# The recurrence's products pA of two heads, issued in turn into two PSUM tiles

## The chip, the cores and the metric

The kernel runs on one core of one Trainium2 chip. The metric is the time of one execution in device microseconds, the median of several runs; the profiled execution is one more run of the same program. Engines are named as in the profile: PE is TensorE (PEld its weight loads), DVE is VectorE, ACT is ScalarE, POOL is GpSimd and SP is SyncE, which issues the DMAs.

## The reference, cut to what matters

A block of a model with 512 tokens and 1024 channels: a gated feed-forward, a mixer with two branches (an RWKV-7 recurrence with 16 heads of 64, and dilated attention), a second feed-forward, then two more layers of another kind. The change lies in the recurrence, which the reference writes as a scan over the tokens:

```
def step(state, inp):
    r_t, w_t, k_t, v_t, a_t, b_t = inp
    sa = jnp.einsum('bhvk,bhk->bhv', state, a_t)
    state = (state * w_t[:, :, None, :] + sa[..., None] * b_t[:, :, None, :]
             + v_t[..., None] * k_t[:, :, None, :])
    return state, jnp.einsum('bhvk,bhk->bhv', state, r_t)
```

The kernel computes it by chunks of 64 tokens. Within a chunk, all products of the rows (a, r) with the rows (b, k) are needed, masked to the past tokens: this is the matrix A of the chunk, and the part of it that belongs to a and b is inverted.

## The kernel before, in words

The 16 heads are worked in 8 pairs j; a pair's two heads lie on partitions 0 to 63 and 64 to 127 of the same tiles. The 512 tokens are 8 chunks c. In the mixer (`rwkv`, line 1179) five generators run beside one another:

- `rw_chunks` (line 1443), the recurrence itself: for each pair and chunk the short products po, pu, pS and po again, with copies on ACT and an add on DVE between them.
- `rw_solve` (line 1397), the inverse of each chunk's matrix: it loads the masked products through a DRAM tile scrA into AS, runs 31 rows of a DVE multiply (pr) and a DVE sum (Tt), writes the result through scrT, and ends with the products pZ and pW.
- `rw_prep` (line 1269), which makes each pair's operands; the change is here.
- `rw_stream` and `rw_fill` (lines 1241 and 1255), the projections prj of 128x512, three products for each block of weights, which fill TensorE. The norms of attention's q and k (ssq, bcq, pt) hang on them.

A generator's `yield` names the engine that its next step wants. `drive` (line 438) chooses, in a first pass over the program, which generator goes next: the one whose engine is free soonest by a clock of estimated costs (`Clock`, line 192), plus a priority (0 for the recurrence, 300 for the inverse, 600 for the preparation, 2000 and 5000 for the projections). The clock takes a 128-column float32 product at 4 x 128 columns of 2.4 GHz and prices one after the other. The order found is recorded and replayed; a scheduler below it places the instructions on the engines and adds all waits. Each engine runs its instructions in the written order.

In `rw_prep`, BK holds the rows b and k and AR the rows a and r of a pair, 128 partitions with 8 chunks of 128 columns. From line 1345 on the loops run over the head h, then over the half q of the chunks. A step makes the products of four chunks of one head into one PSUM tile pA (128x512, one of the two buffers of tag g, line 1274), and a step on DVE multiplies it by the mask into AA. Tag g also holds pz, pa, pl, psk, prn, pb, pv and pbt of the preparation and ssq, bcq and pt of attention's norms. After the fourth multiply, SP issues the DMAs to scrA and TB (lines 1356 to 1359) and the flag A (line 1362) lets the inverse of the pair begin. From the third pair on, the block waits until the recurrence is done with the pair before the last (line 1340).

Attention, later in the kernel, has products of the same form in `att_block` (line 1119): s is made for the two heads of a pair, from partitions 0 to 63 and from 64 to 127, each into its own PSUM tile.

Of the kernel before, what the change touches and what calls it, by code (L numbers as in the profile page):

```python
# [13 lines left out]
P = 128  # L14
# [513 lines left out]
class K:  # L528
# [740 lines left out]
    def rw_prep(self, j, tw, lad):  # L1269
        nc, t1, t2 = self.nc, self.t1, self.t2  # L1270
# [3 lines left out]
        g = lambda sh, nm: self.rps["g"].tile(sh, F32, tag="g", name=nm)  # L1274
        tri, bd, mask = self.rcon["tri"], self.rcon["bd"], self.rcon["rwmask"]
# [48 lines left out]
        AR = t1.tile([P, 8, P], F32, tag="AR", name="AR")  # L1324
        BK = t1.tile([P, 8, P], F32, tag="BK", name="BK")
# [17 lines left out]
        AAs = AA.rearrange("p h c t -> p (h c) t")  # L1343
        R["AR"] = AR
        pend = None
        for h in range(2):
            p0 = 64 * h
            for q in range(2):
                pA = g([P, 4, P], "pA")
                for x in range(4):  # L1350
                    c = q * 4 + x
                    nc.tensor.matmul(pA[:, x], BK[p0:p0 + 64, c], AR[p0:p0 + 64, c], start=True, stop=True)
                yield "DVE"
                nc.vector.tensor_mul(AA[:, h, q * 4:q * 4 + 4], pA, mask.unsqueeze(1).to_broadcast([P, 4, P]))
                yield "PE"
        for b in range(2):
            nc.sync.dma_start(self.scrA[j][b].rearrange("s j i -> j s i"), AAs[b * 32:b * 32 + 32, :, b * 32:b * 32 + 32])
        R["TB"] = TB = t2.tile([64, 16, P], F32, tag="TB", name="TB")
# [1138 lines left out]
```

## Time and profile before

| | us |
|---|---|
| median of 3 runs | 2564.78 |
| lowest and highest run | 2545.41, 2572.88 |
| the profiled execution | 2555.58 |
| its span, first to last instruction | 2553.8 |
| mean granted TensorE clock, share of full speed | 0.948 |

The page of the profile gives for each engine the busy time and its share of the span, and for 40 equal slices of the span the busy share. The chain of waits is the work that ended last, followed back from the last instruction. A group of instructions has its count, its busy time in us and the mean of one in ns, then the idle time of its engine before it and what ended it. A float32 product shows as two records, each with its weight load.

### The profile page before, as it was taken

How to read it: one execution, taken by the hardware profiler on the slowest of the kernel's cores; microseconds unless marked ns; L12 is line 12 of the kernel's file. 1: busy time of each engine (PE TensorE's matmuls, PEld its weight loads, DVE VectorE, ACT ScalarE, POOL GpSimd, SP SyncE). 2: the span in 40 equal slices, each digit the busy share in tenths (PEclk: the TensorE clock that was granted, in tenths of full speed). 3: DMA queues.
4: the chain of work that ended last, by engine and by line, in shares of the span. 5: the costliest groups of instructions: out<-in, count | busy, mean ns of one | idle time of the engine just before them, and what ended most of it. 6: DMA issues, size and time to landing. Idle time of an engine off the chain costs nothing.

```text
span 2553.8 us, 33817 instructions
## 1 busy us (share of the span) xinstructions
PE 2372.9 (93%) x12556; PEld 1920.0 (75%) x12556; DVE 1703.2 (67%) x3157; ACT 1014.7 (40%) x1852; POOL 745.1 (29%) x441
## 2 busy tenths in 40 slices
PE   8798999999999999989989899999889999789897
PEld 6576887877777777757878788888677778677776
DVE  8999357676666656534767846664559865568865
ACT  4212224334233333335433533333335655345553
POOL 4444443010111110212423233335332332232331
PEclk9998999999889869979999999999899999899998
DMA  6555323433223224332423232433310222310221
GB/s 210 188 199 180 100 95 107 121 86 102 79 56 105 66 56 117 130 121 79 127 96 113 82 128 74 145 109 112 128 61 25 71 63 67 116 47 26 64 78 53
DMA packets 122196, 254.24 MB, mean 100 GB/s; under 512 B 39208, under 2 KB 54576, under 8 KB 121392
## 3 DMA queue, kind: packets, MB, share of 16 engines
q1 hardware_dynamic: 122032, 252.09, 31.6%
q8 instruction: 99, 1.62, 0.3%
q14 instruction: 65, 0.53, 0.1%
HBM read 222.07 MB, written 21.59 MB: 95 GB/s over the span
## 4 chain that ended last, share of the span: by engine, by line
PE 68%; DVE 19%; ACT 4%; issue 4%; DMA 2%; POOL 2%; SPq 0%; DVEq 0%; ACTq 0%; POOLq 0%
PE prj L318 12%; PE po L318 11%; PE pj L318 7%; PE pu L318 6%; PE pg L318 6%; DVE mjunk L318 5%; PE pm L318 4%; PE pwo L318 4%; PE sc L318 3%; PE pt L318 2%; DVE c0cy L318 1%; DVE fb L318 1%; PE pA L318 1%; DMA wm<-in_l_mod 1%; PE pl L318 1%
## 5 line engine op out<-in xcount | busy, mean ns | idle before, releaser
L318 POOL TENSOR_TENSOR wlo<-wraw,whi 128x1024 fp32r<-128x1024 f32 (+5 forms) x239 | 552.3, 2312 | 1012.6 <-ACT whi L318 926.4
L318 ACT CAST whi<-wraw 128x1024 fp32r<-128x1024 f32 (+4 forms) x330 | 324.8, 984 | 584.3 <-PE po L318 110.7
L318 PE MATMUL prj<-HH,whi 128*128 128x512 f32 x464 | 197.4, 426 | 0.0
L318 PE MATMUL prj<-HH,wlo 128*128 128x512 f32 x464 | 190.9, 412 | 0.0
L318 PE MATMUL prj<-HL,whi 128*128 128x512 f32 x464 | 187.4, 404 | 0.0
L318 DVE SCALAR_TENSOR_TENSOR mjunk<-wm,cc 128x1024 f32<-128x1024 f32 x96 | 165.5, 1724 | 6.1 <-DMA wm<-in_l_mod 4.7
L318 PE MATMUL po<-FH,whi 128*128 128x512 f32 x352 | 141.1, 401 | 13.2 <-ACT FH L318 13.1
L318 DVE TENSOR_TENSOR wlo<-wraw,whi 128x512 fp32r<-128x512 f32 (+1 forms) x149 | 122.5, 832 | 41.6 <-ACT whi L318 35.8
L318 PE MATMUL pu<-HH,wlo 128*128 128x512 f32 x352 | 139.0, 401 | 11.9 <-POOL wlo L318 11.9
L318 PE MATMUL pg<-HH,whi 128*128 128x512 f32 x352 | 139.5, 396 | 8.2 <-ACT HH L318 7.3
L318 PE MATMUL pu<-HH,whi 128*128 128x512 f32 x352 | 141.4, 402 | 1.3 <-ACT whi L318 1.3
L318 PE MATMUL po<-FL,whi 128*128 128x512 f32 x352 | 140.2, 398 | 0.8 <-DVE FL L318 0.8
L318 PE MATMUL po<-FH,wlo 128*128 128x512 f32 x352 | 139.8, 397 | 1.1 <-POOL wlo L318 1.1
L318 PE MATMUL pu<-HL,whi 128*128 128x512 f32 x352 | 140.2, 398 | 0.0
L318 PE MATMUL pg<-HL,whi 128*128 128x512 f32 x352 | 139.0, 395 | 0.5 <-DVE HL L318 0.5
L318 PE MATMUL pg<-HH,wlo 128*128 128x512 f32 x352 | 135.8, 392 | 1.1 <-POOL wlo L318 1.1
L318 DVE TENSOR_TENSOR ptl<-pt,pth 128x512 fp32r<-128x512 f32 x156 | 105.1, 685 | 36.3 <-ACT pth L318 35.3
L318 PE MATMUL pj<-HH,whi 128*128 128x512 f32 (+1 forms) x304 | 123.2, 409 | 3.2 <-ACT HH L318 3.2
L318 POOL TENSOR_TENSOR se<-SV,EC 64x128 f32<-64x128 f32 x56 | 36.3, 648 | 302.4 <-DVE SV L318 238.8
L318 PE MATMUL pj<-HL,whi 128*128 128x512 f32 (+1 forms) x304 | 123.4, 407 | 0.6 <-DVE HL L318 0.6
L318 PE MATMUL pj<-HH,wlo 128*128 128x512 f32 (+1 forms) x304 | 123.7, 408 | 0.0
L318 ACT ACTIVATE pr<-sc,am 128x768 f32<-128x768 f32 (+1 forms) x120 | 98.0, 818 | 58.7 <-DVE am L318 54.4
(745 smaller groups left out, 5974.2 us busy)
## 6 DMA issues: line engine op xcount, KB each, us to landing
wraw<-in_ffn_w SPq DMA_DIRECT2D x96, 512.0 KB, 3.3
wm<-in_l_mod SPq DMA_DIRECT2D x48, 512.0 KB, 3.5
wraw<-in_l_b SPq DMA_DIRECT2D x45, 512.0 KB, 3.4
wraw<-in_w_rkv SPq DMA_DIRECT2D x24, 512.0 KB, 3.7
wraw<-in_w_qkv SPq DMA_DIRECT2D x18, 512.0 KB, 3.3
wraw<-in_w_gate SPq DMA_DIRECT2D x16, 512.0 KB, 3.9
wraw<-in_ffn_w SPq DMA_DIRECT2D x16, 448.0 KB, 3.4
xd<-X SPq DMA_DIRECT2D x24, 256.0 KB, 3.0
```

Source lines behind the costliest of these rows:

```text
L318: r = real(*a, **kw)
```

## The change

The loop over the halves q becomes the outer one. Two tiles pA are taken together, one for each head; the products of a chunk are issued for head 0 and then head 1, chunk by chunk; then two steps on DVE multiply the two tiles. All operands, tiles and shapes stay as they are.

```
-        for h in range(2):
-            p0 = 64 * h
-            for q in range(2):
-                pA = g([P, 4, P], "pA")
-                for x in range(4):
-                    c = q * 4 + x
-                    nc.tensor.matmul(pA[:, x], BK[p0:p0 + 64, c], AR[p0:p0 + 64, c], start=True, stop=True)
+        for q in range(2):
+
+            pAs = [g([P, 4, P], "pA") for h in range(2)]
+            for x in range(4):
+                c = q * 4 + x
+                for h in range(2):
+                    p0 = 64 * h
+                    nc.tensor.matmul(pAs[h][:, x], BK[p0:p0 + 64, c], AR[p0:p0 + 64, c], start=True, stop=True)
+            for h in range(2):
                 yield "DVE"
-                nc.vector.tensor_mul(AA[:, h, q * 4:q * 4 + 4], pA, mask.unsqueeze(1).to_broadcast([P, 4, P]))
-                yield "PE"
+                nc.vector.tensor_mul(AA[:, h, q * 4:q * 4 + 4], pAs[h], mask.unsqueeze(1).to_broadcast([P, 4, P]))
+            yield "PE"
```

## Rows read from the trace of the kernel before

**Rows 1.** The page, busy time of each engine over the span
```profile
PE 2372.9 (93%) x12556; PEld 1920.0 (75%) x12556; DVE 1703.2 (67%) x3157; ACT 1014.7 (40%) x1852; POOL 745.1 (29%) x441
```

**Rows 2.** By stretch: length, busy PE, PEld, DVE, ACT, POOL, clock, DMA share, GB/s
```profile
460.00:1076.00 616.00, 594.80 (x3486) 462.11 (x3485) 392.96 (x1185) 209.60 (x413) 76.29 (x87) 0.91 0.31 87
900.00:972.00 72.00, 66.78 (x403) 52.63 (x403) 43.08 (x137) 22.24 (x54) 9.77 (x14) 0.76 0.22 58
```

**Rows 3.** The chain of waits from 460 to 972 us, shares by line
```profile
by line: PE prj L318 41.4%; PE po L318 8.2%; PE pA L318 5.7%; PE pu L318 3.8%; PE pS L318 3.3%; DVE pr L318 2.7%; PE ssq L318 2.6%; PE pb L318 2.1%; PE pgg L318 1.9%; DVE Tt L318 1.9%; DVE wlo L318 1.8%; issue 1.7%; PE pa L318 1.6%; PE pl L
```

**Rows 4.** Groups of instructions of TensorE from 460 to 972 us, pA
```profile
L318 PE MATMUL pA<-AR,BK 64*128 64x128 f32 x256 | 42.9, 312 | 4.5 <-DVE BK L318 2.4 <-DVE AA L318 2.0
```

**Rows 5.** Timeline of TensorE (start us, length us, what), two blocks of pA
```profile
646.31 1.16 PE L318 MATMUL pA<-AR,BK 64*128 64x128 f32 x8
647.40 0.43 PE L318 MATMUL po<-SV,AA 128*128 128x64 f32 x2
...
754.92 2.05 PE L318 MATMUL pA<-AR,BK 64*128 64x128 f32 x16
756.90 0.50 PE L318 MATMUL prj<-HH,whi 128*128 128x512 f32 x1
```

**Rows 6.** Timeline of TensorE, attention's products s: two heads, then one
```profile
1149.36 0.72 PE L318 MATMUL s<-kT,qT 64*128 64x128 f32 x8
1150.01 0.50 PE L318 MATMUL pm<-HH,wlo 128*128 128x512 f32 x1
...
1155.99 0.71 PE L318 MATMUL s<-kT,qT 64*128 64x128 f32 x4
1156.63 0.50 PE L318 MATMUL pm<-HH,wlo 128*128 128x512 f32 x1
```

**Rows 7.** Busy time by stretch, as in Rows 2: the clock around three blocks
```profile
754.90:756.90 2.00, 2.00 (x17) 1.86 (x17) 0.93 (x3) 1.98 (x3) 0.00 (x0) 1.00 0.00 0
1149.30:1150.10 0.80, 0.80 (x11) 0.62 (x9) 0.68 (x2) 0.80 (x4) 0.00 (x0) 1.00 0.00 0
906.30:910.40 4.10, 4.03 (x17) 3.53 (x16) 2.88 (x6) 0.89 (x2) 0.20 (x1) 0.50 0.12 17
```

**Rows 8.** Timeline, the block of pA at 906.28 us
```profile
906.28 4.21 PE L318 MATMUL pA<-AR,BK 64*128 64x128 f32 x16
```

**Rows 9.** Instructions on tile pA: the multiplies, ns min/median/max, first and last start
```profile
L318 DVE TENSOR_TENSOR AA<-pA,c_rwmask x32: 669/684/694, 471.3 to 971.0; 128x512 f32<-128x512 f32 x32
```

**Rows 10.** Timeline around the first and the third pair's multiplies
```profile
471.29 1.28 DVE L318 TENSOR_TENSOR AA<-pA,c_rwmask 128x512 f32<-128x512 f32 x2
...
472.03 2.31 PE L318 MATMUL pA<-AR,BK 64*128 64x128 f32 x16 [0.52 <-DVE AA L318]
...
579.02 0.93 PE L318 MATMUL pA<-AR,BK 64*128 64x128 f32 x6
...
603.09 1.29 DVE L318 TENSOR_TENSOR AA<-pA,c_rwmask 128x512 f32<-128x512 f32 x2 [2.98 <-PE po L318]
...
604.22 0.71 PE L318 MATMUL pA<-AR,BK 64*128 64x128 f32 x4
```

**Rows 11.** Busy time by stretch: first, last and sum of five at low clock
```profile
473.70:477.10 3.40, 3.40 (x11) 2.04 (x10) 1.59 (x3) 0.00 (x0) 0.00 (x0) 0.50 0.25 68
...
746.80:753.50 6.70, 6.70 (x25) 5.08 (x25) 3.65 (x10) 0.94 (x4) 1.18 (x2) 0.50 0.42 141
sum 23.60, PE 22.18 PEld 15.97 DVE 17.08 ACT 2.19 POOL 1.18; mean PE 4.44 PEld 3.19 DVE 3.42 ACT 0.44 POOL 0.24
```

**Rows 12.** Timeline of pZ, first and last of eight; groups of DVE, 460 to 972 us
```profile
549.05 1.13 PE L318 MATMUL pZ<-AS,TB 32*32 32x32 f32 x30
1064.01 1.16 PE L318 MATMUL pZ<-AS,TB 32*32 32x32 f32 x31
...
L318 DVE TENSOR_TENSOR pr<-Tt,AS 128x2 f32<-128x2 f32 (+30 forms) x210 | 75.0, 357 | 4.6
L318 DVE TENSOR_REDUCE Tt<-pr 128x1 f32<-128x2 f32 (+30 forms) x209 | 51.1, 245 | 4.4
```

## The prediction

> **What bounds the kernel now.** I read the page first: over the 2553.8 us span TensorE matmul is busy 93%, VectorE 67%, ScalarE 40% [rows 1]. The products pA lie only between 469 and 970 us, so the second view is the table by stretch. From 460 us to 1076 us, where the last projection of this stage ends, TensorE is busy 594.8 of 616 us and idle for 21 us; VectorE is busy 393 us [rows 2]. In the part from 900 to 972 us the share is lower (66.8 of 72 us) and the granted clock is 0.76. The third view, the chain of waits cut to 460 to 972 us, shows what that busy engine is worth: the projections prj hold 41.4% of the chain, po 8.2%, pA 5.7%, and the VectorE rows of the inverse, pr and Tt, 2.7% and 1.9% [rows 3]. TensorE in its written order is the bound of this stage, and pA is on its path for 5.7% of 512 us = 29.2 us. The groups of instructions put the busy time of all 256 pA records at 42.9 us [rows 4]. The code has 8 pairs of heads x 2 heads x 8 chunks = 128 products, so each is two records.
>
> **The change part by part.** *Added and removed instructions: none.* The 128 products, the 32 mask multiplies and the DMAs of the block stay as they are. What changes is the order, which PSUM buffers are held together, and the steps the planner sees.
>
> *Products in turn.* Today a step issues four products of one head. The timeline shows sixteen records of one head from 754.92 to 756.90 us = 1.98 us until the next instruction, and eight from 646.31 to 647.40 us = 1.09 us; the difference over eight is 0.111 us a record [rows 5]. What do two heads cost that alternate? Attention's products s have the same shape (64 rows, 64x128 moving) and take both halves of the rows into two PSUM tiles. Eight of them, four of each head, stand from 1149.36 to 1150.01 us = 0.65 us; four of a single head, from 1155.99 to 1156.63 us, take 0.64 us [rows 6]. So a second head costs nothing there: the two halves run side by side. The granted clock is 1.00 in the stretches at 754.9 and at 1149.3 us, so these compare like with like [rows 7]. Sixteen records of two heads are eight slots: 0.65 + 4 x 0.111 = 1.09 us, against 1.98 us. That is 0.89 us less for each of 16 groups of sixteen: 14.2 us. At granted clock 0.50 (the 2.4 GHz engine at 1.2 GHz) sixteen records take 4.21 us, a short wait in them included [rows 7, 8]; about two and a half of the 16 groups lie there and save some 0.85 us more each: 2 us, 16.3 us in all. Bounds from both sides: nothing if the halves do not overlap, 21.4 us if all 42.9 us halve. What counts is the path. Half of the chain's 29.2 us is 14.6 us, close to the 14.2 us of the groups; I take 14.5 us.
>
> *The buffers.* Both tiles of a step now come from tag g, which has two. Today the second tile's products lie over the first tile's multiply, and the third tile waits for the first multiply alone. Afterwards the second step's two heads wait for both multiplies. A multiply takes 0.685 us [rows 9]. In the timeline of the first pair, two multiplies start at 471.29 us and the next products at 472.03 us with 0.52 us of idle; for the third pair the first two tiles' products end at 579.95 us, their multiplies run from 603.09 to 604.38 us, and the next products start at 604.22 us, between them other work keeps TensorE busy [rows 10]. Half of the eight pairs are as tight as these two; each would be late by one more multiply: 4 x 0.7 = 2.8 us. Bounds: nothing, if the planner puts projections there as it does now, and for eight pairs both multiplies with a handoff of about 0.2 us on either side (1.8 us each), 14 us. I take 2.8 us, nearest to the two rows.
>
> *A rule that speaks against it.* The row says that two multiplies take 1.37 us, longer than the 1.09 us that sixteen paired products would. The Trainium skill, TensorEngine Tiling (Array Packing), section PSUM Bottleneck, says that tiling quickens TensorE but not the emptying of PSUM, which may then be the limit. By that rule the 32 multiplies, 21.9 us, would set the pace instead of 16 x 1.98 = 31.7 us, and the gross gain would be 9.8 us and not 14.2 us. By the rows of the third pair the multiplies lie far from their products with other TensorE work between, so I keep the larger sum.
>
> *The step order.* Eight alternations of TensorE and VectorE steps become two steps of eight products with two multiplies after each. Head 1's first products move ahead of head 0's second. The scrA and TB DMAs on SP and the inverse still wait for the last multiply, and no POOL work is moved. But the recorded plan, which prices eight products as eight in a row and knows nothing of the overlap, will be another for the whole stage. No row prices that. The idle time of TensorE in the stage, 21 us [rows 2], bounds what a better order can win, and I take the same for a worse one; value zero.
>
> *How much carries through.* TensorE is 97% busy, but at each handoff (po, copy, pu, copy, pS) it waits for others, and a shorter TensorE stretch turns partly into waits. I keep 0.8 of the net: 0.8 x (14.5 - 2.8) = 9.4 us. Bounds are none and all of it.
>
> *Clock.* Five stretches at granted clock 0.50 begin on, or within 1 us after, a block of pA products, 23.6 us in sum [rows 11]. The engine was near fully busy in them, so at full clock about half, 11.8 us, would go. Whether denser products keep the clock up no row tells; I take 2 us and leave the rest as a rival.
>
> Sum: 9.4 + 2 = 11.4 us, so the profiled execution would go from 2555.58 to 2544.2 us. The median of the runs, 2564.78, is 9.2 us above that execution; kept, it gives 2553 us.
>
> **The rivals.** *The clock stays up too.* All 11.8 us come: 9.4 + 11.8 = 21.2 us, 2543.6 us. For it: five blocks of half-empty products stand next to the falls. Against: low clock also falls where the recurrence's short products run, as from 900 to 972 us.
>
> *The inverses set the pace.* Their pZ products start at 549.05 us for the first pair and at 1064.01 us for the last, seven steps of 73.6 us each [rows 12]. If the inverse with its VectorE rows and DMAs paces the stage, TensorE only waits longer, and no more than the tail of 2 us is won: 2563 us. Against: pr and Tt hold 4.6% of the chain, prj 41.4%.
>
> *No overlap.* For the third pair the sixteen products of one head were cut into pieces of 4, 6 and 6 records with recurrence products between; the last piece is in [rows 10]. If the written order separates the heads, nothing is saved and the longer wait remains: 2564.8 + 2.8 = 2568 us.
>
> *Slower: the seam in a pair.* Both buffers of tag g are held until two multiplies are done, and everything else that uses the tag (pb, pv, pz, pa, the norms of q and k) queues behind. If VectorE's order puts these multiplies behind rows of the inverse (0.357 + 0.245 us for one of its 31 rows [rows 12]), as it did for 23 us in the third pair, and TensorE's order has the second step before the filling projections, TensorE stands. It waits in order, so the recurrence behind it stands too. It decides from 14.5 / 8 = 1.8 us a pair. With ten inverse rows, 6 us, at each of eight seams: 48 - 14.5 = 33 us, 2598 us.
>
> **How the numbers follow.** Chances: forecast 0.50, clock 0.20, inverses pace 0.13, no overlap 0.05, seam 0.12. A measurement of this kernel tells about 1% from no change, 25.6 us. Faster by over that needs the clock rival with a kinder plan (0.10 of its 0.20), or a kind plan in the forecast (0.09 of 0.50): 0.19. Slower by over 1% is the seam in most of its cases and hardly anything else: 0.09. The rest, 0.72, lies within. For eight in ten the range goes down to the clock rival with some 17 us of the plan's 21 us (2527 us) and up past "no overlap" by 8 us (2576 us); what is left out is most of the seam above and a very good plan below.
>
> **What would show it.** Right: 256 pA records again, but sixteen of two heads until the next instruction in about 1.1 us at full clock, busy time of the group near 22 to 26 us, its chain share in this stretch near 3%, VectorE's 32 multiplies unchanged at 0.685 us, and the last projection of the stage some 10 us earlier. Wrong: pA records still 0.111 us apart (no overlap); pZ still 73.6 us apart with more TensorE idle than 21 us (inverses pace); TensorE waits for the mask multiply well above 5 us in sum (seam). The forecast itself falls if the stage's end moves by another amount than pA's busy time explains, which would be the new plan or the clock.

## The result, and the profile after

The changed kernel takes 2581.24 us (median of 20 runs, 2570.81 to 2604.05); in the same comparison the kernel before takes 2554.55 us (20 runs, 2542.92 to 2576.46). The ratio is 1.0094 with a 95% interval of 1.0066 to 1.0122: slower by about 24 us (the medians alone are 26.7 us apart), where the forecast was 11.4 us faster and its range ended at 2576 us. The three runs shown ahead of the prediction had a median 10 us above that of these 20; the ratio goes by the 20. The profiled execution takes 2590.40 us with a span of 2588.6 us, 34.8 us longer than before, at a mean granted clock of 0.932 instead of 0.948.

The page of the changed kernel, which answers to [rows 1]: busy time of the engines, then the granted clock (PEclk, in tenths of full speed) in 40 slices of the span, 65 us each.
```profile
PE 2398.7 (93%) x12556; PEld 1935.6 (75%) x12556; DVE 1710.2 (66%) x3157; ACT 1015.1 (39%) x1854; POOL 739.9 (29%) x441
...
PEclk9999999989777776999999999999899999899998
```
The same line of the page of the kernel before:
```profile
PEclk9998999999889869979999999999899999899998
```
The count of TensorE's instructions is the same, 12556, yet they are busy for 25.8 us more. The clock line says where: in the slices from 10 to 15 (counted from 0), some 650 to 1040 us, it stands at 7 and 6, where before it is 8 or 9 but for one 6.

First the part that the change is about. The groups of instructions from 460 to 1000 us, TensorE's pA (against [rows 4]) and VectorE's multiplies:
```profile
L318 PE MATMUL pA<-AR,BK 64*128 64x128 f32 x256 | 34.9, 342 | 0.3 <-DVE AA L318 0.3
...
L318 DVE TENSOR_TENSOR AA<-pA,c_rwmask 128x512 f32<-128x512 f32 x32 | 21.4, 684 | 8.7 <-PE po L318 4.8 <-PE pA L318 3.9
```
The timeline of TensorE after the change (start us, length us): the first block of pA, and then the block of products pZ with which each of the eight inverses ends:
```profile
469.32 1.16 PE L318 MATMUL pA<-AR,BK 64*128 64x128 f32 x16
470.42 0.50 PE L318 MATMUL prj<-HH,whi 128*128 128x512 f32 x1
...
547.25 1.19 PE L318 MATMUL pZ<-AS,TB 32*32 32x32 f32 x32
621.71 1.19 PE L318 MATMUL pZ<-AS,TB 32*32 32x32 f32 x32
698.11 1.91 PE L318 MATMUL pZ<-AS,TB 32*32 32x32 f32 x32
782.27 1.91 PE L318 MATMUL pZ<-AS,TB 32*32 32x32 f32 x32
856.69 1.91 PE L318 MATMUL pZ<-AS,TB 32*32 32x32 f32 x32
933.76 1.91 PE L318 MATMUL pZ<-AS,TB 32*32 32x32 f32 x32 [1.39 <-DVE AS L318]
1003.99 1.91 PE L318 MATMUL pZ<-AS,TB 32*32 32x32 f32 x32 [1.45 <-DVE AS L318]
1079.34 1.19 PE L318 MATMUL pZ<-AS,TB 32*32 32x32 f32 x32
```
Sixteen records of two heads take 470.42 - 469.32 = 1.10 us until the next instruction, where sixteen of one head took 1.98 us [rows 5]: the two halves do run side by side. The group falls from 42.9 to 34.9 us. TensorE waits little for the multiplies, as its waits from 460 to 1090 us show (what waited, for what; us in total, times, longest):
```profile
PE pb L318 <- DVE AA L318: 2.4, 3, 1.3
...
PE pA L318 <- DVE AA L318: 0.3, 1, 0.3
```
In the kernel before the same view has one such row:
```profile
PE pA L318 <- DVE AA L318: 2.0, 2, 1.5
```
So these waits grow by 0.7 us.

Second, the pZ rows tell of the clock too: a block takes 1.19 us where the granted clock is 1.00 (as at 1079 us) and 1.91 us where it is 0.50 (as at 782 us), and five of the eight are long. In the kernel before the eight blocks start at 549.05, 624.66, 697.71, 773.54, 852.05, 920.88, 991.61 and 1064.01 us, and only the one at 852.05 takes 1.91 us. The steps hardly differ, 73.6 us in the mean before [rows 12] and (1079.34 - 547.25) / 7 = 76.0 us after.

What lies between them does differ. The table by stretch after the change (columns as in [rows 2]): from the third pZ to the last, from the last to attention's first products s, and the whole stage.
```profile
698.10:1079.30 381.20, 350.65 (x1925) 265.38 (x1924) 223.48 (x708) 108.94 (x239) 41.82 (x56) 0.77 0.25 67
1079.30:1164.00 84.70, 81.95 (x453) 61.56 (x452) 29.19 (x56) 29.88 (x56) 14.06 (x11) 0.98 0.42 134
440.00:1164.00 724.00, 683.09 (x3756) 521.80 (x3755) 426.61 (x1251) 232.48 (x461) 84.14 (x99) 0.84 0.30 85
```
The same three stretches of the kernel before:
```profile
697.70:1064.00 366.30, 354.25 (x2084) 272.99 (x2084) 227.13 (x696) 121.70 (x254) 45.23 (x56) 0.88 0.30 85
1064.00:1122.70 58.70, 46.61 (x289) 31.47 (x289) 16.28 (x35) 19.99 (x43) 16.43 (x12) 0.88 0.31 105
440.00:1122.70 682.70, 649.42 (x3759) 500.20 (x3758) 420.85 (x1250) 234.16 (x461) 90.55 (x100) 0.90 0.32 90
```
And the first two for the projections prj alone (busy PE, PEld, DVE, ACT of instructions on this tile), after:
```profile
698.10:1079.30 381.20, 158.61 (x552) 109.11 (x552) 4.42 (x6) 17.84 (x29) 0.77 0.25 67
1079.30:1164.00 84.70, 56.33 (x217) 38.64 (x216) 0.00 (x0) 6.83 (x10) 0.98 0.42 134
```
and before:
```profile
697.70:1064.00 366.30, 196.97 (x720) 135.20 (x720) 6.70 (x9) 21.88 (x34) 0.88 0.30 85
1064.00:1122.70 58.70, 12.19 (x49) 8.70 (x48) 0.00 (x0) 2.06 (x3) 0.88 0.31 105
```
Here is where the time came from. Attention begins 41.3 us later (1164.0 against 1122.7 us). The whole span is only 34.8 us longer, but what follows attention's start varies by more than these 6.5 us: two profiles of the kernel before, the second of which is met below, differ there by 8.5 us. Of the 41.3 us, 14.9 lie between the third and the last pZ, which hold 168 projection products *fewer*, and 26.0 behind the last pZ, where these 168 now stand: 217 records against 49, in a place where nothing but one pair's recurrence is left to lie beside them. Over the whole stage TensorE runs the same instructions (3756 and 3759 records) and is busy 33.7 us longer and idle 7.6 us longer. With two levels, 1.00 and 0.50, a mean of 0.84 over 724 us is 232 us at the low one, and 0.90 over 682.7 us is 137 us.

The changed lines move no projection. The written order does: the planner put its steps in another order. The count of prj products in each interval between inverses, in program order, first to last (up to the first pZ, between two, behind the last):
```
before   312  180  132  134  178   72  132  204   48
after    336  158  130  120   96   72   72  192  216
```
Intervals with 72 products and with 204 take about the same time (before: 68.8 us with 72, 72.4 us with 204; after: 77.1 and 70.2 us with 72, 75.4 us with 192). In the timeline the projections start 0.23 us apart at full clock, so 132 of them are some 30 us of TensorE's work (an estimate from these rows), and an interval without them is shorter by a few us or not at all. A projection taken out of an interval is thus hardly a gain there; it is work left for the end.

### The profile page after: what moved, and what is told of

Same layout as the page of the kernel before. It is cut to its first block, busy times and chain, and to the rows that moved or that the text cites. A ratio compares the mean times of both kernels' runs of the same rounds, so it can differ in the third digit from the quotient of the medians.

```text
span 2588.6 us, 33828 instructions
## 1 busy us (share of the span) xinstructions
PE 2398.7 (93%) x12556; PEld 1935.6 (75%) x12556; DVE 1710.2 (66%) x3157; ACT 1015.1 (39%) x1854; POOL 739.9 (29%) x441
## 4 chain that ended last, share of the span: by engine, by line
PE 36%; DVE 9%; ACT 3%; issue 2%; POOL 2%; DMA 0%; SPq 0%; DVEq 0%; POOLq 0%; ACTq 0%
PE pj L318 7%; PE po L318 6%; PE pwo L318 4%; PE pg L318 4%; PE pu L318 3%; PE pm L318 3%; PE sc L318 3%; PE pt L318 2%; DVE c0cy L318 1%; PE ss L318 1%; DVE X L318 1%; ACT whi L318 1%; DVE x1cy L318 1%; PE pq L318 1%; DVE fb L318 1%
## 5 line engine op out<-in xcount | busy, mean ns | idle before, releaser
L318 POOL TENSOR_TENSOR se<-SV,EC 64x128 f32<-64x128 f32 x56 | 28.6, 511 | 353.9 <-DVE SV L318 314.9
L318 DVE TENSOR_TENSOR ptl<-pt,pth 128x512 fp32r<-128x512 f32 x156 | 105.1, 685 | 36.4 <-ACT pth L318 34.8
```

Of the source, the lines that this page charges most:

```text
L318: r = real(*a, **kw)
```

## The experiments

Theory A (plan): the overlap is worth what was forecast, and the loss comes from the order that the planner finds when a step has eight products priced one after the other. Rivals: B, the paired products themselves make the clock fall; C, the two tiles held together cost waits; D, the inverses set the pace so that nothing done to TensorE counts. Every ratio is against the kernel before, measured in the same comparison; the comparisons ran on different chips, so between two of them ratios are set side by side.

**The old plan with the new products, and the new plan with the old ones.** The first kernel goes through the old loops (head, half, four products, one multiply) in the planner's first pass and issues the paired products, four old steps each with its own yield, when the order is replayed (cut; lines against the changed kernel):
```
+        if self.plan.recording:
...
+        else:
             for q in range(2):
                 pAs = [g([P, 4, P], "pA") for h in range(2)]
...
                 for h in range(2):
                     yield "DVE"
                     nc.vector.tensor_mul(AA[:, h, q * 4:q * 4 + 4], pAs[h], ...)
-            yield "PE"
+                    yield "PE"
```


> The recorded order of steps is that of the kernel before, and the products are issued in turn as in the change. In TensorE's written order 48 projections prj stand behind the last inverse's pZ, as before the change (216 with the change). Theory A (the new order of steps puts the projections late, and the overlap itself is good): faster than before by 6 to 16 us, ratio 0.994 to 0.998, pA busy near 25 us, low clock in the mixer no longer than before. Theory B (products on both halves lower the granted clock): slower than before by 15 to 30 us like the change, ratio 1.006 to 1.012, with over 200 us at clock 0.50 between 460 and 1130 us. Theory C (both buffers of tag g held at once delay the norms and so the projections): slower than before, between the two.

The second keeps the change's steps, prices and two tiles, but a step issues the eight products of one head (cut):
```
+            for h in range(2):
+                p0 = 64 * h
+                pAs = [g([P, 4, P], "pA") for q in range(2)]
+                for q in range(2):
+                    for x in range(4):
+                        c = q * 4 + x
+                        nc.tensor.matmul(pAs[q][:, x], BK[p0:p0 + 64, c], AR[p0:p0 + 64, c], ...)
```


> The steps, their prices and the two tiles taken together are those of the change, but a step makes eight products of one head, so no two can overlap. 144 projections stand behind the last pZ. Theory A: slower than before by 15 to 40 us, ratio 1.006 to 1.016, pA records 0.111 us apart. Theory B: no slower than before, ratio 0.997 to 1.003, since no pair of halves runs. Theory C: as slow as the change, 1.006 to 1.012, since both buffers are held here too; A and C are told apart by the first run.

The first took 2559.55 us, ratio 1.0017 (0.9990 to 1.0045); the second 2611.95 us, 1.0238 (1.0215 to 1.0262). The loss goes with the steps and not with the pairs. In size both miss: the first was to be 0.994 to 0.998, the second at most 1.016. The written orders are also not quite those of the two kernels. The second has 325, 167, 132, 120, 96, 72, 86, 250 and 144 products prj in its intervals, so it doesn't yet give the overlap's price; the first has 336, 146, 142, 156 and 156 in its first five, and then the counts of the kernel before. The groups of instructions of the first kernel, pA from 440 to 1130 us:
```profile
L318 PE MATMUL pA<-AR,BK 64*128 64x128 f32 x256 | 28.8, 308 | 2.0 <-DVE BK L318 1.9
```
With the old plan pA falls from 42.9 to 28.8 us, by 14.1 us, and the last pZ begins at 1053.7 us, 10.3 us earlier than before. That the total shows nothing of it is taken up below.

**The order alone, with the old products.** If the order is at fault, the kernel before must become as slow when its projections are put later and nothing else is touched. One number, the priority of the filling projections:
```
-RW_PRIO = {"stream": 2000, "fill": 5000}
+RW_PRIO = {"stream": 2000, "fill": 6000}
```


> The kernel before, with the priority number of the filling projections at 6000 in place of 5000, nothing else. In TensorE's written order 216 projections stand behind the last pZ, as many as with the change. Theory A: slower than before by 20 to 45 us, ratio 1.008 to 1.018, with the low clock between 460 and 1130 us over 200 us, though products, buffers and steps of the block are the old ones. Theories B and C: same as before, ratio 0.997 to 1.003.

And the changed kernel must get back with its projections put earlier:
```
-RW_PRIO = {"stream": 2000, "fill": 5000}
+RW_PRIO = {"stream": 2000, "fill": 4500}
```


> The changed kernel, with the priority number of the filling projections at 4500 in place of 5000, nothing else. No projection stands behind the last pZ. Theory A: the loss goes and the overlap's gain shows: faster than before by 5 to 25 us, ratio 0.990 to 0.998; less would be left if the recurrence's tail now stands alone. Theory B: slow like the change, 1.006 to 1.012, since the products still run on both halves. Theory C: slow like the change too.

The kernel before with late projections took 2590.68 us, 1.0149 (1.0119 to 1.0179). Its table by stretch, third to last pZ, whole:
```profile
695.80:1083.40 387.60, 358.68 (x1952) 275.36 (x1951) 224.56 (x710) 112.37 (x243) 42.71 (x56) 0.78 0.26 71
```
and on prj alone, with the stretch up to attention:
```profile
695.80:1083.40 387.60, 166.81 (x576) 115.99 (x576) 4.43 (x6) 19.73 (x32) 0.78 0.26 71
1083.40:1169.90 86.50, 56.28 (x217) 38.64 (x216) 0.00 (x0) 6.87 (x10) 0.98 0.43 138
```
This is the picture of the change, without the change: 576 projections where there were 720, clock 0.78, 217 left behind the last pZ. So rivals B and C aren't needed for the loss: products and buffers here are the old ones. The changed kernel with early projections took 2555.93 us, 1.0004 (0.9976 to 1.0033), no product prj behind the last pZ, and this row from its third to its last pZ:
```profile
711.40:1078.50 367.10, 353.25 (x2094) 265.33 (x2093) 231.09 (x688) 124.09 (x257) 55.76 (x59) 0.89 0.32 91
```
The same 367 us and the same clock as before the change. The loss is gone, but the gain that was expected beside it (0.990 to 0.998) doesn't show. This is the row from its last projection to attention:
```profile
1030.50:1133.50 103.00, 75.41 (x348) 50.80 (x346) 34.40 (x99) 19.65 (x54) 14.67 (x17) 0.55 0.16 51
```
With no projection left for the end, TensorE is busy 75 of 103 us there at a clock of 0.55, and attention begins at 1133.5 us, 10.8 us later than in the kernel before.

**The price told to the planner.** If a wrong price made the order, the right one should mend it. The planner's clock is told that head 1's product costs nothing beside head 0's:
```
-                    c = 4 * max(n, m) / 2.4
+                    c = 0.0 if clk.half else 4 * max(n, m) / 2.4
...
+                    self.clk.half = h
                     nc.tensor.matmul(pAs[h][:, x], BK[p0:p0 + 64, c], AR[p0:p0 + 64, c], ...)
+            self.clk.half = 0
```


> The changed kernel; the clock of estimated costs that orders the steps counts head 1's product of each two at nothing, as it runs beside head 0's. No projection stands behind the last pZ then, 72 before it, and 167 and 192 in the two stretches before. Theory A: the loss of 24 us goes; with the tail of the recurrence alone at the end as in the run with earlier filling, 0.996 to 1.002 against before. Theory B: slow like the change, 1.006 to 1.012.

It took 2551.37 us, 0.9990 (0.9961 to 1.0019): the loss is gone. The row on prj alone between its third and last pZ:
```profile
699.80:1059.60 359.80, 195.65 (x708) 132.94 (x708) 5.94 (x8) 22.05 (x34) 0.91 0.33 94
```
708 projections lie there again, and five steps take 359.8 us, 72.0 us each, at a clock of 0.91. In the profile its attention begins at 1114.8 us, 7.9 us earlier than in the kernel before, which is about what the ratio's interval leaves unseen. What its end costs shows in the whole row from the last projection to attention:
```profile
1019.40:1114.80 95.40, 67.33 (x346) 45.24 (x344) 34.36 (x99) 19.61 (x54) 14.84 (x17) 0.61 0.17 55
```
No projection is left for the last stretch, the granted clock there is 0.61, and TensorE stands idle for 28 us. This run shows that an order with the projections earlier takes the loss away, as the earlier fill did by another number; that it is the truth of the price and not only the order that it leads to is not shown.

**The overlap alone, in an order that doesn't move.** Both heads' products are issued as in the change but read the same half of the rows (head 1's products use head 0's data), so that nothing can overlap and every engine keeps its written order. The traces of each pair of kernels show the same sequence of instructions on TensorE, VectorE and ScalarE. Once in the change:
```
                 for h in range(2):
-                    p0 = 64 * h
+                    p0 = 0
```


> The changed kernel, with head 1's products reading head 0's partitions (0 to 63) in place of its own, so that all products of the block use one half of the array's rows and none can overlap; head 1's matrix A is head 0's. The written order of all five engines is the same as that of the changed kernel, instruction for instruction. Overlap worth its time (theory A): slower than the changed kernel by 8 to 16 us, so 1.012 to 1.016 against before; pA records 0.111 us apart. Overlap lowers the clock (theory B): faster than the changed kernel, under 1.007. Overlap hidden (its 14 us turn into waits): within 5 us of the changed kernel, 1.007 to 1.011.

and, by the same edit, in the kernel with the old plan:

> The same substitution (head 1's products read head 0's partitions) in the kernel with the old order of steps and products in turn, whose order of instructions it keeps exactly. That kernel came to 1.0017 against before. Theory A: slower than it by 8 to 16 us, so 1.005 to 1.008. Hidden in the recurrence's tail: the last pZ some 10 us later, but the whole within 5 us of it, 1.000 to 1.004.

In the change's order it took 2605.72 us, 1.0197 (1.0147 to 1.0247). Its timeline, its group pA and its table by stretch:
```profile
473.85 2.05 PE L318 MATMUL pA<-AR,BK 64*128 64x128 f32 x16
475.83 0.50 PE L318 MATMUL prj<-HH,whi 128*128 128x512 f32 x1
```
```profile
L318 PE MATMUL pA<-AR,BK 64*128 64x128 f32 x256 | 47.3, 335 | 0.3 <-DVE AA L318 0.3
```
```profile
704.50:1095.40 390.90, 360.78 (x1925) 274.62 (x1924) 222.58 (x708) 108.87 (x239) 41.84 (x56) 0.75 0.24 66
```
Sixteen records take 1.98 us again, and the clock is as low as in the change (0.75 against 0.77). So the order and the two tiles together cost about 50 us (1.97% of 2554.55 us; the interval, from six runs, leaves 38 to 63 us), and the overlap gives back 24.5 us by the medians, more than the 8 to 16 us expected; 12.4 us of it is pA's own busy time, and in the traces attention begins 17.7 us earlier with it (1164.0 against 1181.7 us). The two intervals don't touch. TensorE waits for the multiplies for under 3 us in both, which speaks against C, as does the first kernel, which holds both tiles too and loses nothing; and the clock is no higher without the overlap, which rules out B.

In the old plan's order the same edit took 2549.63 us, 0.9983 (0.9952 to 1.0014), against 1.0017 with the overlap: no gain from the overlap, if anything the other sign, where at least 1.000 had been expected. Yet the last pZ begins at 1053.7 us with the overlap and at 1061.5 us without, 7.8 us apart (some 10 us were expected). What follows differs. The stretch from the last projection to attention with the overlap:
```profile
1068.60:1125.10 56.50, 47.31 (x168) 29.81 (x166) 11.15 (x28) 11.33 (x29) 8.91 (x9) 0.54 0.22 78
```
and without it:
```profile
1076.30:1120.30 44.00, 31.98 (x166) 19.68 (x164) 11.21 (x28) 11.37 (x29) 10.71 (x10) 0.84 0.32 115
```
The same last pair's recurrence, alone on TensorE, runs with some 52 of 56.5 us at the low clock in the one and 14 of 44 us in the other: 12.5 us lost, the 7.8 us won and more. To see whether that is chance, the kernel before was run once more, unchanged:

> The kernel before, unchanged, for a second profile: how long the low clock lasts in the mixer (150 us between 460 and 1130 us in the first) and in the tail behind the last projection (14 us of 44 us). Ratio 0.998 to 1.002. If the tail shows some 40 us at clock 0.50 here too, the first profile's tail was a kind one, and the 10 us that the run with old steps and products in turn is ahead at the last pZ are not given back there; if again near 14 us, they are.

It took 2550.38 us, 0.9994 (0.9955 to 1.0032), with its last pZ at 1063.9 us and the same picture in the tail as without the overlap, some 14 of 43.6 us at the low clock. So without the overlap the tail is short in each of the three profiles; of the kernel with the overlap there is one, and what made its clock fall so soon behind its last projection is open.

**The tail's clock.** If the gain is lost in a tail at the low clock, then keeping TensorE busy there should bring it out. In the last pair's recurrence, after each of its three steps per chunk, two products of 128 columns are added whose results nobody uses, 48 in all (cut; the same call stands behind the second step):
```
+        def more(x):
+            if j == 7 and not self.plan.recording:
+                p = self.rps["g"].tile([P, T], F32, tag="g", name="junk")
+                k = x.shape[0]
+                for i in range(2):
+                    nc._nc.tensor.matmul(p[:, i * P:(i + 1) * P], self.ident[0:k], x, start=True, stop=True)
...
+            more(SV[:, c])
             yield "ACT"
```
This was put into the old plan with pairs, and into the change with the right price:

> The kernel with the old order of steps and products in turn, and in the recurrence of the last pair two further products of 128x128 behind each of its three steps in a chunk, 48 in all, whose results are not used. They read what the step has just used, so they stand where TensorE waits for the copies. In that kernel's profile the last pZ came 7.8 us before that of the same order on one half, but the tail behind the last projection took 56.5 us, 51.8 of them at clock 0.50, against 44.0 us with 14.4 us. Theory A with a tail that lost its clock: the added work keeps the clock up, tail 42 to 48 us, and the 8 us show: ratio 0.994 to 0.999 against before, where it was 1.0017. Rival (the tail is paced by handoffs, the clock there is of no account): the added work, 48 x 0.22 us = 10.6 us, is partly on the path: 1.002 to 1.006.

> The same 48 unused products in the changed kernel with its estimated costs mended, where no projection stands behind the last pZ: there the stretch from the last projection to attention's first product took 95 us, 75 of them at clock 0.50, and the whole came to 0.999. Theory: with the clock up in the last pair's recurrence, 10 to 25 us less: 0.990 to 0.995. Rival: handoffs pace the tail, 0.999 to 1.003. The added products begin with the last pair's first chunk, so the stretch from 1020 to 1060 us stays thin in both cases.

and then, to part the overlap from the added products, into the old plan with one half and into the kernel before:

> The kernel with old steps, products in turn and the filled tail (0.9941), but with head 1's products on head 0's partitions, so that nothing overlaps; the written order of all engines is the same. Overlap worth its 8 us once the tail keeps its clock: slower than that kernel by 6 to 14 us, 0.996 to 0.9995. Overlap of no account (the gain is the filled tail's alone): 0.993 to 0.995.

> The kernel before with the same 48 unused products in the last pair's recurrence. Its tail lost its clock late (14 us of 44 us), so there is less to win: 0.995 to 1.000, and the kernel with products in turn and the filled tail is ahead of it by 6 to 14 us. If the filled tail is all, it comes to 0.993 to 0.995 as well.

The old plan with pairs and a filled tail took 2539.14 us, 0.9941 (0.9916 to 0.9967): faster than the kernel before and the changed one. The stretch from its last pZ to attention, then the same for one half and for the kernel before, each with the added products:
```profile
1054.60:1110.80 56.20, 51.80 (x374) 40.66 (x373) 17.50 (x35) 18.93 (x42) 14.12 (x11) 1.00 0.34 109
```
```profile
1061.40:1117.70 56.30, 51.75 (x372) 40.62 (x372) 17.52 (x35) 18.89 (x42) 14.13 (x11) 1.00 0.36 113
```
```profile
1066.50:1121.60 55.10, 51.72 (x372) 40.63 (x372) 17.49 (x35) 18.88 (x42) 14.11 (x11) 1.00 0.33 106
```
All three tails are at full clock and take 55 to 56 us, and the three kernels differ by the start of the tail. One half took 2550.82 us, 0.9974 (0.9939 to 1.0009), the kernel before 2550.67 us, 0.9977 (0.9949 to 1.0005). At one and the same written order the kernel with the overlap is thus 0.33%, some 8 us, ahead of the one without. The intervals of these two ratios overlap, and 0.33% is less than their uncertainty together, so the times alone don't show it. Two pairs of traces, one profile of each kernel, do: with the overlap the last pZ begins 6.8 us earlier here and 7.8 us earlier without the added products, and attention begins 6.9 us earlier here (1110.8 against 1117.7 us). The added products alone give the kernel before nothing that can be told from no change: it had only some 14 us of low clock in its tail to win back.

With the right price instead of the old plan, the filled tail took 2568.75 us, 1.0052 (1.0026 to 1.0078), where 0.990 to 0.995 was expected: a miss. The clock fell some 6 us behind the last projection, ahead of all but two of the added products. The row of the stretch up to attention, and the same in two parts, before and after the fall:
```profile
1021.10:1140.30 119.20, 98.97 (x438) 71.97 (x437) 34.38 (x99) 19.63 (x54) 15.10 (x17) 0.52 0.14 45
1021.10:1026.80 5.70, 3.42 (x22) 2.20 (x21) 5.50 (x14) 2.41 (x5) 4.36 (x2) 1.00 0.74 282
1026.90:1140.30 113.40, 95.54 (x416) 69.77 (x416) 28.79 (x86) 17.22 (x49) 10.75 (x15) 0.50 0.11 34
```
Ahead of the fall TensorE was busy for 3.4 of 5.7 us. Here the same 48 products didn't bring the clock back: it stayed low, and attention begins 25.5 us later than without them (1140.3 against 1114.8 us). So a low clock in the end of this order is seen, but that keeping TensorE busy mends it is not shown for this order, and why the clock stayed low with TensorE busy 95.5 of 113.4 us is open.

## Why the prediction was wrong

**Products in turn: right.** 1.09 us was forecast for sixteen records of two heads, 1.10 us is measured. Of the 14.5 us taken for all blocks, 42.9 - 28.8 = 14.1 us came with the old plan; against the same order on one half, where the group is 42.0 us, it is 13.2 us. In the change itself the group is 34.9 us, not 22 to 26 us, since more of it lies at the low clock; the sign "22 to 26 us" was too low in every order that was run, 28.6 us at the least.

**The buffers: small, as was said, but not 2.8 us.** 2.8 us were set down as added delay; the waits for the multiplies are 2.4 + 0.3 = 2.7 us, but 2.0 us of such waits stood there before, so 0.7 us were added. The upper bound of 14 us rested on a handoff of 0.2 us on either side; behind a multiply the trace shows 0.05 us. The seam inside a pair, the slower rival with 2598 us, didn't happen: attention's start is late, but not by waits for a multiply. The Trainium skill, TensorEngine Tiling (Array Packing), section PSUM Bottleneck, says that the emptying of PSUM may become the limit. The trace shows no such limit here: the multiply is 0.684 us as before [rows 9], and the block of pA shown above is followed by a projection and not by a wait. The 4.4 us that the prediction worked out for that case were rightly left in the gain.

**The step order: this is the step that failed.** It was valued at zero, within 21 us either way, because TensorE is idle for 21 us in the stage [rows 2] and no order can win more than that. For a loss this is no bound. A worse order doesn't only add idle time: it moved 168 projections from intervals whose length they hardly set to the end, where they do count, and the thinner intervals ran at a lower clock, 0.77 in place of 0.88. With the overlap taken out and the order kept, the cost is 1.97%, 50 us; the priority of the projections alone makes the kernel before slower by 1.49%; the old plan, the right price and an earlier fill each bring it back to 1.00. The text's own last sign was the one that appeared: pA's busy time fell by 8.0 us and attention moved by 41.3 us the other way, "which would be the new plan or the clock"; it was both. It had said that the plan "prices eight products as eight in a row and knows nothing of the overlap" and would be another "for the whole stage", and then gave it no sign, and as its size the idle time, which bounds the wrong side.

**How much carries through: neither 0.8 nor a constant.** In the change's order the overlap gives 24.5 us by the medians, above pA's own 12.4 us; with the old plan and the tail filled some 7 us by the traces; with the old plan alone nothing that shows. There the one profile has the tail at the low clock, and filling the tail brings the gain out; why the tail's clock fell is open.

**Clock: wrong sign.** 2 us were counted as a gain from a higher clock. The stage has some 232 us at the low clock instead of 137.

**The rivals.** Neither "no overlap" (2568 us) nor a clock that stays up (2543.6 us) came true. That the inverses set the pace was given 0.13 and 2563 us, argued from 73.6 us between pZ. The step is indeed near that with 72 or 204 projections in it, and after the change pZ waits for VectorE at two of its eight blocks; but what follows is not that TensorE doesn't matter. Rival and forecast look like two sides of one stage: the inverses largely set how long an interval lasts, TensorE's order sets how much of its work fits in, and what is left is paid at the end. This is a reading of the intervals; no run made the inverses faster or slower. It isn't the whole of it either: with the right price the last interval, with 72 projections, took 62.5 us. The change then splits into order and tiles, some +50 us, and overlap, -24.5 us; that the two add up to the measured change follows from how they were measured and is no check.

How thin an interval must be for the clock to fall isn't settled by these runs. From the third to the last pZ they show 0.75 to 0.78 in each of the four profiles in which projections had been moved out to the end, and 0.87 to 0.91 in the others.

## What to carry to other kernels

When a change makes instructions cheaper inside a program that a cost model orders, change the price in the model in the same edit, and compare the written order of before and after ahead of any time: here one price was worth 1%, and an order with the projections late cost more than the overlap gave. To measure an overlap, take it away without touching the order, by letting both parts use the same rows. A stage's idle time bounds what a better order wins, not what a worse one loses.

## What was not expected of the hardware

Products on the two halves of the rows overlapped as far as the records can show: sixteen in 1.10 us, where eight of one half take 1.09 us [rows 5], so that the change of PSUM tile from one product to the next costs nothing that shows.

The clock can take back a gain made elsewhere: in the old plan the stage's last stretch got 12.5 us longer after a start 7.7 us earlier, with the same instructions, by some 52 in place of 14 us at the low clock. Products with no use kept it at 1.00 over 55 to 56 us in the tails of three kernels; in a fourth, where it had fallen before nearly all of them, the clock was 0.52 over 119 us with them.
